# A hybrid encoder layer: where the second product of the fourth and fifth gathered tiles is made

## The chip, the cores and the metric

The kernel runs on one core of a Trainium2 chip. The metric is the device time of one execution in microseconds; the median of three runs of the kernel before is 4287.37 us.

## What is computed

An encoder layer is applied with shared weights to 256 prompt tokens and 1024 sample tokens (width 1024). A recurrent branch and an attention branch are merged; then a channel mixer with product keys picks, for each token, 8 heads x 16 = 128 of 16384 experts. Only the mixer matters here; a tile is 128 tokens.

```python
u = jnp.take(u_tab, eidx, axis=0)      # (128 tokens, 8, 16, 1024)
ve = jnp.take(v_tab, eidx, axis=0)
act = gelu(einsum('td,thkd->thk', zt, u)) * g
return einsum('thk,thkd->td', act, ve)
```

The first product (`u`) gives 128 numbers for each token; the second (`ve`) is a sum of 128 rows weighted by them. The mixer's result is added to the residual and normalised.

## The kernel before

The ten tiles of tokens take two ways through the mixer. Six are gathered: each of a token's 128 expert rows is fetched by index. These are the two prompt tiles (`rP`, here tiles 1 and 2), the first two sample tiles (`r0`, tiles 3 and 4) and the last two (`r1`, tiles 5 and 6). The other four sample tiles (`rd`, 512 tokens) are dense: `weights` (line 1016) turns their picks into a full table of weights, by small matmuls (lines 1034 and 1053), and `dense` (line 1063) multiplies the 512 tokens with all 16384 experts in 128 blocks, 48 fp32r matmuls of 512 columns to a block (lines 140 to 142). `second` adds its results to `acc` on VectorE (line 1096), and `load_split` divides every loaded table block in a high and a low part on ScalarE and VectorE (lines 123 and 124).

For a gathered tile:

- `u_steps`: 128 steps. Each issues one indirect DMA of 512 KB on GpSimd's queue (line 938) and one dot product on VectorE (line 940, with a small read of the accumulator).
- `v_steps`, second product on TensorE: 128 indirect DMAs (line 969); after every fourth, one group of 8 fp32 matmuls (16 records in the trace) with a 128x32 selector that holds the weights (line 976), into `acc` in PSUM. Before it, the 128x128 weights are transposed on TensorE (line 954).
- `v_slots`, the same on VectorE: after every DMA (line 994) one multiply-add of 128x1024 (line 996). A route with the key `"acc"` takes this way. It yields after every second DMA.

All these tiles, and `gffn`, `gfin`, `y` and `x2r`, share one ring of 7 buffers (`ring`, line 925), handed out in the order of the program text; a gather can be issued when the buffer seven back is free. `experts` pairs the second product of a tile with the first of the next one:

```python
def experts(routes):
    prev = None
    for r in routes + [None]:
        us = u_steps(r) if r else iter(())
        vs = (v_slots if "acc" in prev else v_steps)(prev) if prev else iter(())
        while us or vs: ...          # one step of each in turn
        prev = r
```

A scheduler puts the instructions of all stages on each engine's queue when the program is built, by a timeline of its own and with the text's order as priority; the steps of the second product have a higher one. Each engine then runs its queue strictly in that order. So the gathers, which come after `merge` in the text, run beside the attention and merge stages, and those of tiles 5 and 6 beside `weights` and `dense`.

Of the kernel before, what the change touches and what calls it, by code (L numbers as in the profile page):

```python
# [50 lines left out]
def encoder(ctx, tc, I, O, dbg=None):  # L51
# [876 lines left out]
    def u_steps(route):  # L928
        tt, gw, ei = route["tt"], route["gw"], route["ei"]
        zs = pe_.tile([P, D], F32, name="zs", tag="zs")  # L930
        nc.gpsimd.dma_start(zs, x2d[tt:tt + P])
        gffn = ring("gffn")
        nc.sync.dma_start(gffn, I["norm_ffn"].partition_broadcast(P))
        nc.vector.scalar_tensor_tensor(out=zs, in0=zs, scalar=route["rt"], in1=gffn, op0=OP.mult, op1=OP.mult)
        dots = pe_.tile([P, P], F32, name="dots", tag="dots", bufs=2)
        for s in range(P):
            ug = ring("ug")
            nc.gpsimd.indirect_dma_start(out=ug, out_offset=None, in_=I["peer_u"],  # L938
                                         in_offset=bass.IndirectOffsetOnAxis(ap=ei[:, s:s + 1], axis=0))
            nc.vector.scalar_tensor_tensor(out=ug, in0=ug, scalar=1.0, in1=zs, op0=OP.mult, op1=OP.mult,  # L940
                                           accum_out=dots[:, s:s + 1])
            yield
        act = pe_.tile([P, P], F32, name="act", tag="act", bufs=2)
        nc.scalar.activation(out=act, in_=dots, func=AF.Gelu)
        nc.vector.tensor_tensor(act, act, gw.rearrange("p h k -> p (h k)"), op=OP.mult)
        route["act"] = act
        yield
# [162 lines left out]
# [5 lines that stand above are left out]
            while us or vs:  # L1115
                if us and next(us, "end") == "end":
                    us = None
                if vs:
                    with tc.high_priority():
                        if next(vs, "end") == "end":  # L1120
                            vs = None
            prev = r
# [82 lines left out]
    r0 = []  # L1205
# [24 lines left out]
    tctx.close()  # L1230
    rd, r1 = rs[:ND // P], rs[ND // P:]
    vp = ctx.enter_context(tc.tile_pool(name="VA", bufs=1, side="right"))
    for r in r1:
        r["acc"] = vp
    experts(r0 + r1)
    acc = ctx.enter_context(tc.tile_pool(name="DA", bufs=1, side="left")).tile([P, ND // P, D], F32, name="acc")
    up = ctx.enter_context(tc.tile_pool(name="DU", bufs=1, side="left"))
    dense(rd, zt, acc, up, up0, psum_pool(ctx, "psS", 3, "left"), psum_pool(ctx, "psV", 3, "left"))
# [77 lines left out]
```

## Time and profile before

| | |
|---|---|
| median of 3 runs | 4287.37 us (4286.51 to 4300.59) |
| profiled execution | 4300.6 us, span 4298.8 us |
| TensorE busy | 3802.2 us, 88% of the span |
| VectorE busy | 3234.1 us, 75% |
| GpSimd busy | 1818.6 us, 42% |
| ScalarE busy | 1559.9 us, 36% |
| DMA | 1263.92 MB, mean 294 GB/s |

The profiled execution is the slowest of the three by 13 us. Busy shares are means over stages with different limits; the stage of `dense` fills the last 1.5 ms. A matmul's listed duration overlaps with the next one's, so a count of matmuls in a stretch tells its rate better than the busy time.

### The profile page before, as it was taken

The numbers are of one execution on the slowest core, as the hardware profiler recorded it, in microseconds if no ns is written. First come the engines' busy times: TensorE is split into PE (matmuls) and PEld (weight loads), VectorE is DVE, ScalarE is ACT, GpSimd is POOL, SyncE is SP. The second block draws the span as 40 slices with busy tenths as digits, with TensorE's granted clock in tenths as the row PEclk, the third lists the DMA queues.
The fourth block names the chain that finished last, engine by engine and source line by source line (L and its number), as shares of the span: only waits on it lengthen the run. The fifth ranks groups of instructions, "written<-read, shape, count | busy, mean of one in ns | idle before, by whom it ended". The sixth has DMA issues, their size and how long they took to land.

```text
span 4298.8 us, 55005 instructions
## 1 busy us (share of the span) xinstructions
PE 3802.2 (88%) x18206; PEld 2734.5 (64%) x18206; DVE 3234.1 (75%) x8002; ACT 1559.9 (36%) x2600; POOL 1818.6 (42%) x1565
## 2 busy tenths in 40 slices
PE   6998999997777988877988489999999999899998
PEld 5777777775434753345644155677777877777786
DVE  4637988567988773986679985567668999999954
ACT  5555455454233214431201187522222222222232
POOL 0000644334444343774545512344446556666500
PEclk9999999998888999888999688999999999999999
DMA  5455899889999987998988847899999999999941
GB/s 160 123 183 152 324 344 343 315 305 319 318 311 313 323 312 272 328 339 326 334 293 285 292 181 292 325 322 339 334 333 356 339 358 362 365 364 346 326 140 64
DMA packets 508318, 1263.92 MB, mean 294 GB/s; under 512 B 49920, under 2 KB 203136, under 8 KB 505984
## 3 DMA queue, kind: packets, MB, share of 16 engines
q0 software_dynamic: 224352, 816.94, 52.9%
q1 hardware_dynamic: 197056, 354.05, 24.2%
q10 hardware_dynamic: 86624, 89.40, 6.1%
q8 instruction: 144, 2.36, 0.2%
q14 instruction: 142, 1.16, 0.1%
HBM read 1165.05 MB, written 95.16 MB: 293 GB/s over the span
## 4 chain that ended last, share of the span: by engine, by line
PE 55%; DMA 13%; DVE 12%; issue 12%; ACT 4%; POOL 2%; SPq 0%; another core or an unknown queue 0%; POOLq 0%; ACTq 0%; DVEq 0%
PE pm L140 12%; PE pm L141 11%; PE pm L142 11%; PE pm L138 7%; DMA vg<-peer_v,eit 5%; PE acc L976 5%; DVE ug L940 4%; DMA ug<-peer_u,ei 3%; PE pm L1053 3%; POOL ug L938 1%; PE pm L1034 1%; PE pm L437 1%; DVE vacc L996 1%; POOL vg L969 1%; PE pm L624 1%
## 5 line engine op out<-in xcount | busy, mean ns | idle before, releaser
L938 POOL DMA_INDIRECT ug<-peer_u,ei x768 | 908.9, 1184 | 800.8 <-DVE ug L940 334.2
L940 DVE SCALAR_TENSOR_TENSOR ug<-ug,zs 128x1024 f32<-128x1024 f32 x768 | 931.5, 1220 | 252.6 <-DMA ug<-peer_u,ei 189.3
L969 POOL DMA_INDIRECT vg<-peer_v,eit x512 | 540.7, 1056 | 752.8 <-DVE ug L940 308.9
L994 POOL DMA_INDIRECT vg<-peer_v,ei x256 | 354.7, 1385 | 207.0 <-DVE vacc L996 120.3
L141 PE MATMUL pm<-vl,ah 128*128 128x512 f32 x1024 | 405.1, 397 | 22.8 <-DVE vl L124 22.8
L140 PE MATMUL pm<-zth,uh 128*128 128x512 f32 x1024 | 406.3, 397 | 8.7 <-ACT ge L1080 6.0
L142 PE MATMUL pm<-zth,ul 128*128 128x512 f32 x1024 | 405.2, 396 | 0.0
L141 PE MATMUL pm<-ztl,uh 128*128 128x512 f32 x1024 | 404.8, 395 | 0.0
L976 PE MATMUL acc<-vg,zt 128*32 128x512 f32 x2048 | 284.6, 679 | 133.7 <-DMA vg<-peer_v,eit 132.8
L142 PE MATMUL pm<-vh,al 128*128 128x512 f32 x1024 | 400.6, 394 | 0.0
L140 PE MATMUL pm<-vh,ah 128*128 128x512 f32 x1024 | 374.9, 398 | 11.3 <-DVE acc L1096 5.5
L996 DVE SCALAR_TENSOR_TENSOR vacc<-vg,act,vacc 128x1024 f32<-128x1024 f32 x256 | 327.7, 1280 | 3.0 <-DMA vg<-peer_v,ei 0.9
L138 PE MATMUL pm<-xg,wraw 128*128 128x256 f32 (+1 forms) x1024 | 295.2, 441 | 4.1 <-DVE sr L855 4.1
L123 ACT CAST uh<-uraw 128x1024 fp32r<-128x1024 f32 x128 | 134.5, 1051 | 432.5 <-PE pm L141 413.2
L123 ACT CAST vh<-vraw 128x512 fp32r<-128x512 f32 x256 | 157.5, 618 | 352.0 <-DMA vraw<-peer_v 257.3
L140 PE MATMUL pm<-hh,wh 128*128 128x512 f32 x672 | 269.9, 402 | 5.0 <-ACT gt L240 3.0
L141 PE MATMUL pm<-hl,wh 128*128 128x512 f32 x672 | 268.3, 399 | 0.0
L142 PE MATMUL pm<-hh,wl 128*128 128x512 f32 x672 | 266.3, 396 | 0.0
L138 PEld LDWEIGHTS pm<-xg,wraw 128*128 128x128 f32 x1024 | 193.2, 194 | 80.6 <-issue 56.9
L141 PEld LDWEIGHTS pm<-vl,ah 128*128 128x128 f32 x1024 | 194.0, 189 | 75.1 <-DVE vl L124 31.5
L140 PEld LDWEIGHTS pm<-vh,ah 128*128 128x128 f32 x1024 | 194.1, 190 | 66.4 <-DVE acc L1096 14.1
L140 PEld LDWEIGHTS pm<-zth,uh 128*128 128x128 f32 x1024 | 192.2, 188 | 64.6 <-ACT ge L1080 11.4
(368 smaller groups left out, 7502.1 us busy)
## 6 DMA issues: line engine op xcount, KB each, us to landing
uraw<-uT SPq DMA_DIRECT2D x128, 512.0 KB
vraw<-peer_v SPq DMA_DIRECT2D x256, 256.0 KB
wraw<-wi SPq DMA_DIRECT2D x84, 512.0 KB
gd<-gs ACTq DMA_DIRECT2D x16, 2048.0 KB
g<-gd ACTq DMA_DIRECT2D x32, 1024.0 KB
wraw<-wq SPq DMA_DIRECT2D x48, 512.0 KB
wraw<-wo SPq DMA_DIRECT2D x24, 512.0 KB
ug<-peer_u,ei POOLq DMA_INDIRECT x768
```

Of the source, the lines that this page charges most:

```text
L123: nc.scalar.copy(hi, src)
L138: nc.tensor.matmul(out, w[0], x[0], start=start, stop=stop)
L140: nc.tensor.matmul(out, w[0], x[0], start=start, stop=False)
L141: nc.tensor.matmul(out, w[0], x[1], start=False, stop=False)
L142: nc.tensor.matmul(out, w[1], x[0], start=False, stop=stop)
L938: nc.gpsimd.indirect_dma_start(out=ug, out_offset=None, in_=I["peer_u"], in_offset=bass.IndirectOffsetOnAxis(ap=ei[:, s:s + 1], axis=0))
L940: nc.vector.scalar_tensor_tensor(out=ug, in0=ug, scalar=1.0, in1=zs, op0=OP.mult, op1=OP.mult, accum_out=dots[:, s:s + 1])
L969: nc.gpsimd.indirect_dma_start(out=vg, out_offset=None, in_=I["peer_v"], in_offset=bass.IndirectOffsetOnAxis(ap=eit[:, t:t + 1], axis=0))
L976: nc.tensor.matmul(acc[g_ * 32:(g_ + 1) * 32, n * 512:(n + 1) * 512], zt[:, h, g_, i], v_[:, n * 512:(n + 1) * 512], start=b == 0 and i == ...
L994: nc.gpsimd.indirect_dma_start(out=vg, out_offset=None, in_=I["peer_v"], in_offset=bass.IndirectOffsetOnAxis(ap=ei[:, s:s + 1], axis=0))
L996: nc.vector.scalar_tensor_tensor(out=acc, in0=vg, scalar=act[:, s:s + 1], in1=acc, op0=OP.mult, op1=OP.add)
L1053: nc.tensor.matmul(pm[:, j * P:(j + 1) * P], ol[:, j], oh[:, j], start=True, stop=True)
```

## The change

Only the last gathered tile keeps its second product on VectorE, and the list of four tiles is given to `experts` in two calls. Between the calls there is no pairing: tile 4's second product comes alone, then tile 5's first product alone.

```diff
     vp = ctx.enter_context(tc.tile_pool(name="VA", bufs=1, side="right"))
-    for r in r1:
+    for r in r1[1:]:
         r["acc"] = vp
-    experts(r0 + r1)
+    experts(r0)
+    experts(r1)
     acc = ctx.enter_context(tc.tile_pool(name="DA", bufs=1, side="left")).tile([P, ND // P, D], F32, name="acc")
```

The order of the stages of tiles 3 to 6, before: first 3; first 4 with second 3; first 5 with second 4; first 6 with second 5 (VectorE); second 6 (VectorE). After: first 3; first 4 with second 3; second 4; first 5; first 6 with second 5 (TensorE); second 6 (VectorE). All queues are the same up to the end of the second product of tile 3.

GpSimd's queue at that end, before (line 982 and 1014 belong to tile 3's output, line 931 loads tokens for tile 5):

```order
L982 DMA x2r<-x2d 128x1024
L931 DMA zs<-x2d 128x1024
L1014 DMA y<-y 128x1024
L938 DMA ug<-peer_u,ei 128x1024
L969 DMA vg<-peer_v,eit 128x1024
```

The same place after:

```order
L931 DMA zs<-x2d 128x1024
L969 DMA vg<-peer_v,eit 128x1024 x17
L1014 DMA y<-y 128x1024
L969 DMA vg<-peer_v,eit 128x1024 x111
L982 DMA x2r<-x2d 128x1024
L938 DMA ug<-peer_u,ei 128x1024 x10
L1014 DMA y<-y 128x1024
L938 DMA ug<-peer_u,ei 128x1024 x119
```

The alternation of `ug` (tile 5) and `vg` (tile 4) has become one run of 128 `vg` and then one run of `ug`.

VectorE's queue in the middle of `dense`, before, where `ug` is tile 6 and `vacc` tile 5:

```order
L1096 TENSOR_TENSOR acc<-pm,acc 128x512
L996 SCALAR_TENSOR_TENSOR vacc<-vg,act,vacc 128x1024
L1082 TENSOR_TENSOR ge<-ge,g 128x512 x2
L124 TENSOR_TENSOR ul<-uraw,uh 128x1024
L940 SCALAR_TENSOR_TENSOR ug,dots<-ug,zs 128x1024
L996 SCALAR_TENSOR_TENSOR vacc<-vg,act,vacc 128x1024
L160 TENSOR_TENSOR al<-ge,ah 128x512 x2
L124 TENSOR_TENSOR vl<-vraw,vh 128x512
L996 SCALAR_TENSOR_TENSOR vacc<-vg,act,vacc 128x1024
```

After, while tile 5's dot products run alone (this stretch now lies early in `dense`):

```order
L1082 TENSOR_TENSOR ge<-ge,g 128x512
L940 SCALAR_TENSOR_TENSOR ug,dots<-ug,zs 128x1024 x2
L124 TENSOR_TENSOR vl<-vraw,vh 128x512
L160 TENSOR_TENSOR al<-ge,ah 128x512
L940 SCALAR_TENSOR_TENSOR ug,dots<-ug,zs 128x1024
L1082 TENSOR_TENSOR ge<-ge,g 128x512
L124 TENSOR_TENSOR ul<-uraw,uh 128x1024
L124 TENSOR_TENSOR vl<-vraw,vh 128x512
L940 SCALAR_TENSOR_TENSOR ug,dots<-ug,zs 128x1024
```

The 128 multiply-adds of tile 5 are gone from this queue; what stands between the dense operations is one kind of gathered work at a time.

TensorE's queue behind the transposition of tile 4's weights, at the start of `weights`, after the change:

```order
L1053 MATMUL pm<-oh,ol 128x128 x4
L1034 LDWEIGHTS cs
L1034 MATMUL pm<-cbk,cs 128x512
L976 MATMUL acc<-vg,zt_3898 32x512 x8
L1034 LDWEIGHTS cs
L1034 MATMUL pm<-cbk,cs 128x512
L1053 MATMUL pm<-oh,ol 128x128 x4
```

Before, no group of line 976 stands among the first 60 of the 128 such pieces of `weights`, and 6 groups in all of it; after, 17 of tile 4's 32 groups. Tile 5's 32 groups now stand between matmuls of `dense`, where there were none.

## Rows read from the trace of the kernel before

**Rows 1.** The page's slices, 40 equal parts of the span, busy tenths.

```profile
PE   6998999997777988877988489999999999899998
...
DVE  4637988567988773986679985567668999999954
...
DMA  5455899889999987998988847899999999999941
```

**Rows 2.** Tile views: engine, operation, count; least/median/most ns; first and last start.

```profile
L954 PE MATMUL acc<-ident,act x4: 270/302/448, 771.0 to 2484.9; 128*128 128x128 f32 x4
...
L976 PE MATMUL acc<-vg,zt x2048: 592/592/1064, 797.4 to 3242.3; 128*32 128x512 f32 x187
...
L996 DVE SCALAR_TENSOR_TENSOR vacc<-vg,act,vacc x256: 1269/1279/1315, 3252.9 to 4077.7; 128x1024 f32<-128x1024 f32 x128
...
L940 DVE SCALAR_TENSOR_TENSOR ug<-ug,zs x768: 1159/1219/1296, 446.4 to 3789.1; 128x1024 f32<-128x1024 f32 x192
...
L1010 ACT ACTIVATE sq<-vacc x2: 1056/1058/1060, 3657.8 to 4079.0; 128x1024 f32<-128x1024 f32 x2
```

**Rows 3.** Windows of the last six stretches: busy of each engine, PE clock, DMA share, GB/s.

```profile
2490.00:2745.00 255.00, 239.91 (x1391) 152.78 (x1391) 169.21 (x459) 198.95 (x276) 54.62 (x57) 0.93 0.67 252
2745.00:2800.00 55.00, 54.10 (x248) 40.69 (x247) 31.04 (x46) 17.57 (x24) 20.38 (x18) 1.00 0.96 352
2800.00:3200.00 400.00, 398.17 (x1874) 295.46 (x1873) 264.44 (x413) 108.87 (x164) 187.43 (x170) 1.00 0.93 331
...
3300.00:3660.00 360.00, 336.69 (x1413) 265.99 (x1412) 339.72 (x425) 97.17 (x146) 214.69 (x169) 0.98 0.97 354
3660.00:3790.00 130.00, 120.68 (x503) 95.52 (x503) 125.83 (x212) 36.76 (x55) 87.56 (x66) 0.98 0.99 367
3790.00:4080.00 290.00, 282.66 (x1195) 223.31 (x1194) 277.04 (x306) 83.15 (x126) 179.28 (x123) 0.99 0.96 344
4100.00:4260.00 160.00, 160.00 (x697) 130.45 (x696) 75.94 (x105) 48.87 (x74) 0.00 (x0) 1.00 0.33 104
```

**Rows 4.** Windows of line 976 alone, the selector products of the gathered rows.

```profile
2490.00:2745.00 255.00, 11.54 (x96) 2.50 (x96) 0.93 0.67 252
...
2800.00:3200.00 400.00, 40.40 (x336) 8.77 (x336) 1.00 0.93 331
```

**Rows 5.** Timeline of TensorE around one line 976 group: start, length, instruction.

```profile
3146.87 0.39 PE L141 MATMUL pm<-ztl,uh 128*128 128x512 f32 x1
3147.19 1.93 PE L976 MATMUL acc<-vg,zt 128*32 128x512 f32 x16
3149.04 0.50 PE L142 MATMUL pm<-zth,ul 128*128 128x512 f32 x1
3149.38 0.39 PE L140 MATMUL pm<-zth,uh 128*128 128x512 f32 x1
```

**Rows 6.** Waits of TensorE from 3300 to 4080: total us, times, longest.

```profile
PE pm L141 <- DVE vl L124: 22.8, 16, 4.3
PE pm L140 <- ACT ge L1080: 6.0, 6, 1.8
```

**Rows 7.** Window of line 940 alone while dot products run by themselves; two records each.

```profile
3660.00:3790.00 130.00, 77.00 (x127) 0.98 0.99 367
```

**Rows 8.** VectorE groups by line, 3790 to 4080, the last tile's second product.

```profile
L996 DVE SCALAR_TENSOR_TENSOR vacc<-vg,act,vacc 128x1024 f32<-128x1024 f32 x128 | 163.8, 1280 | 1.2
```

**Rows 9.** Waits of TensorE in the weights stretch, 2490 to 2745.

```profile
PE pm L1034 <- DMA cs<-codes: 7.6, 2, 4.5
PE pm L1034 <- ACT gs L1054: 5.6, 5, 4.0
```

**Rows 10.** Waits of TensorE from 1380 to 1700, tile 2's second product alone.

```profile
PE acc L976 <- DMA vg<-peer_v,eit: 25.5, 13, 4.1
```

**Rows 11.** Waits of TensorE from 2490 to 3250.

```profile
PE acc L976 <- DMA vg<-peer_v,eit: 1.8, 1, 1.8
```

**Rows 12.** Waits of TensorE from 1930 to 2490.

```profile
PE acc L976 <- DMA vg<-peer_v,eit: 88.5, 21, 14.9
```

## The prediction

> **What bounds the kernel now.** I read the page's slices first: over the last third TensorE is at 9 tenths nearly everywhere, VectorE climbs to 9 in the slices behind the middle of that third, and the DMA engines are at 9 up to the last three slices [rows 1]. So three resources are nearly full at once, and the question is which one ends each stretch. The tile views date the stretches. Tile 4's weights are transposed at 2484.9 us, its second product on TensorE ends at 3242; the multiply-adds on VectorE run from 3253 to 4078, and the squares of the two finished tiles at 3657.8 and 4079.0 say that tile 5's end near 3660 and tile 6's near 4080; the last dot product is at 3789 [rows 2]. With these dates I asked for a table by stretch [rows 3].
>
> Its last row is the yardstick. From 4100 to 4260 `dense` is alone: 697 matmuls in 160 us, 0.2296 us each, PE never idle. For every other stretch I count the dense matmuls, multiply by 0.2296, and what is left of the stretch is either line 976 or loss.
>
> - 2800 to 3200, tile 5's dot products beside tile 4's second product on TensorE: 1874 records, of which 336 are line 976 [rows 3, 4]. 1538 x 0.2296 = 353.1 us; 46.9 us are left, 1.8 of them idle.
> - 3300 to 3660, tile 6's dot products beside tile 5's multiply-adds: 1413 x 0.2296 = 324.4; lost 35.6 us. VectorE is busy 339.7 of 360.
> - 3660 to 3790, dot products alone: 503 x 0.2296 = 115.5; lost 14.5. VectorE 125.8 of 130.
> - 3790 to 4080, tile 6's multiply-adds alone: 1195 x 0.2296 = 274.4; lost 15.6. VectorE 277.0 of 290 [rows 3].
>
> So TensorE sets the end, and from 3300 to 4080 it loses 65.7 us in all. What it waits for there is VectorE first: 22.8 us for the low part of a table block (line 124), 6.0 for ScalarE's `ge` [rows 6]; the rest of the loss is a clock of 0.98 and short gaps at issue. Before 3300, with the second product on TensorE, nothing is lost.
>
> **The change, term by term.** It adds matmuls to the engine that sets the end and takes work from one that makes it wait; the sum is about these two.
>
> *Tile 5's second product on TensorE: 32 groups of line 976.* Two ways to price one. By the stretch: (398.2 - 353.1) / 21 = 2.15 us, as 336 records are 21 groups of 16. By one group in the timeline: the dense matmul ahead starts at 3146.87, the second one behind it at 3149.38; without the group these two starts would lie 0.46 us apart, they lie 2.51 apart, so the group took 2.05 [rows 5]. I take 2.1: **+67 us** (66 to 69). There is no idle time beside it to hide in, since in its new place, as in 2800 to 3200, TensorE would be at 398 of 400.
>
> Here is the one rule I weigh. The row shows 0.32 us from the last dense start to the group's first, where 0.23 is usual, 1.85 us from the group's start to the next dense start, and 0.34 to the one behind: about 0.2 us of the 2.05 lie at the two borders [rows 5]. The Trainium skill (TensorEngine Tiling (Array Packing), Key Properties) says that a change of the tiling mode, not of the tile alone, drains the engine, and a group of 128x32 among 128x128 matmuls changes it twice. The trace agrees in kind. By the row without its borders 32 groups would be 59 us, with them 67; the rule speaks against the change by those 8.
>
> *Tile 5's multiply-adds leave VectorE.* In the trace, tile 6's take 163.8 us at 1.280 us each [rows 8]; tile 5's are as many. With them goes the mixed stretch. Tile 6's dot products then stand beside line 976, as tile 5's did from 2800 to 3200, where VectorE is busy 264.4 of 400 and TensorE loses nothing. So the 35.6 us of the mixed stretch and the 14.5 us of tile 6's solitary dot products (these are left alone because the multiply-adds go two at a time, so tile 5's are done when tile 6's are halfway) are given back: **-50 us**.
>
> *Tile 5's dot products now come alone, beside dense.* This stretch is new. By the new order it spans some 1246 dense matmuls, 286 us at the full rate. VectorE needs 128 x 1.21 us = 155 for the dots (77.0 us for 63.5 of them, two records each) [rows 7] and, at 75.9 per 160 us [rows 3], 136 for dense, 291 us together: over-full. The nearest rows: dots alone cost 14.5 us per 63.5, that is 29 per 128; multiply-adds alone 15.6 per 128. I take the middle, **+22 us** (15 to 29). Tile 6's own 15.6 us stay as they are: same instructions, same place in dense (blocks 84 to 112 in both orders), with 16 blocks to go behind them.
>
> *Tile 4's second product moves forward.* Before, 6 of its 32 groups lie in `weights` (96 records) [rows 4]; after, 17. 11 x 2.1 = 23 us leave dense and enter `weights`: zero in the sum, except where they fall into idle time. TensorE is busy 239.9 of 255 there [rows 3], waiting 7.6 us for the `cs` load and 5.6 for ScalarE's copy [rows 9]. If TensorE comes later, part of this has arrived; but `cs` and the copy follow from its own progress, so part comes back. Between 0 and 15.1 I take half: **-8 us**. The groups may also wait for their rows, as tile 2's did when its second product ran alone, 25.5 us in 13 waits [rows 10], or hardly, as tile 4's did beside tile 5's dots, 1.8 us [rows 11]. The load on the transfers is nearest to the second: **+5 us**, within 2 to 25. The dots that leave `weights` relieve VectorE, which was at 169 of 255 and not the limit: nothing.
>
> *Small things.* Tile 5's sum of `acc` and residual on VectorE (line 983) is one instruction, about as long as a multiply-add, and the transposition of its weights (line 954, 0.3 us [rows 2]) waits for the last dot product with dense matmuls queued behind it: a few us at most, within the range. DMA: not a byte more or less, the same 256 gathers for each tile; the ring and the two stream borders are as between tiles 1 to 4.
>
> **Sum.** 67 - 50 + 22 - 8 + 5 = **+36 us**. The profiled execution would go from 4300.6 to 4337; it is 13 us over the median, and the same step on the median gives 4287.4 + 36 = **4323 us**. A measurement of this kernel tells about 0.5%, 21 us, from no change; this is 0.8%.
>
> **Rivals.**
>
> *The losses belong to the transfers, not to VectorE: a little faster.* The three lossy stretches have a DMA share of 0.96 to 0.99, the lossless one 0.93 [rows 3], and PE's wait for `vl` has a load in front of it. The change moves 11 groups, 44 gathers of 0.5 MB = 23 MB, into `weights`, where the share is 0.67; at 350 GB/s that is 66 us of transfer out of the full stretches. If this is what counts, neither tile 5's dots nor tile 6's multiply-adds lose anything, and the filled waits of `weights` are worth all 15: 67 - 50 - 16 - 15 = -14 (nothing for tile 5's dots, no 15.6 for tile 6), 4273 us. It decides if the DMA share beside tile 5's dots is under 0.95. Against it: while VectorE is 95% and more busy, the transfers' relief has no room to show, and the named releaser is VectorE's.
>
> *Gathers alone stall TensorE: slower by more.* TensorE's queue is strict, so a group of line 976 whose rows are late stops dense and `weights` too. From 1930 to 2490 it waited so for 88.5 us, 21 times, 4.2 us each [rows 12]. By the new order tile 4's last 15 groups stand some 35 dense matmuls apart; with the group's own time that is 8.0 + 2.1 = 10.1 us for four gathers, 2.5 us each. The transfers have kept up with more: GpSimd's 170 instructions from 2800 to 3200 are one in 2.35 us [rows 3]. So the stretch should hold. If it doesn't, 10 waits of 4.2 us in place of my 5 us give +37 on top: 4360 us. It decides if a gather lands later than 2.5 us behind the one before it, over the length of the stretch.
>
> *The change doesn't do what it says* is ruled out by the order, which shows the moves.
>
> **Chances.** The sum as worked out (4304 to 4340): 0.53, of which 0.08 lies under 4309, within 0.5%. Transfers (4256 to 4300): 0.22, of which 0.08 is faster by over 0.5%. Stalls (4341 to 4375): 0.17. None of these: 0.08, spread as 0.02, 0.03, 0.03. So faster 0.10, same 0.25, slower 0.65. The range leaves out the lower part of the transfers' case and the upper half of the stalls', with the last 0.08 some 0.2: 4268 to 4360. The likeliest case's own range is 4304 to 4340.
>
> **What the profile after would show.** `weights` takes some 15 us longer, with 272 records of line 976 in it. Then tile 5's dots alone, 270 to 310 us long, some 22 us more than its dense matmuls need at 0.2296, with VectorE over 95%. Then about 590 us of tile 6's dots beside line 976, at 470 records per 100 us and no loss. Then tile 6's multiply-adds with some 16 us lost. The forecast is wrong if the second stretch loses nothing or twice as much, if line 976 waits for its gathers in `weights` or early in dense, or if a group costs other than 2.1 us.

## The result and the profile after

The change makes the kernel slower: 4318.99 us, median of 4 runs (4311.5 to 4323.62), beside 4286.94 us for the kernel before (4 runs, 4285.91 to 4300.59), a ratio of 1.0066 with an interval of 1.004 to 1.0091. That is 32 us between the medians, and 28 us (17 to 39) by the ratio. The two profiled executions, 4323.62 and 4300.6 us, are 23 us apart.

From the page of the changed kernel, the busy line and two of the rows by slice, which answer to [rows 1]:

```profile
PE 3837.2 (89%) x18719; PEld 2739.2 (63%) x18719; DVE 3087.6 (71%) x7892; ACT 1560.9 (36%) x2600; POOL 1779.4 (41%) x1565
...
DVE  4637987567987774886679974348886666689964
...
DMA  5464999889999888998987878889989999999951
```

VectorE has 147 us less to do, TensorE 35 more. VectorE's solid run of nines over the last quarter is broken up: three eights (tile 5's dot products alone), five sixes (line 976 beside tile 6's dot products), then an eight and two nines with tile 6's multiply-adds. The transfers stay at 8 or 9 tenths through all of this, up to the last two slices, as before.

The tile views of `vg` in the changed kernel (columns as in [rows 2]): line 976 has 512 records more and ends 573 us later; one tile is left on line 996, and it ends 46 us later.

```profile
L976 PE MATMUL acc<-vg,zt x2560: 592/592/1063, 797.1 to 3815.7; 128*32 128x512 f32 x197
...
L996 DVE SCALAR_TENSOR_TENSOR vacc<-vg,act,vacc x128: 1270/1279/1318, 3824.4 to 4123.6; 128x1024 f32<-128x1024 f32 x128
```

These dates cut the changed kernel into the stretches that the prediction spoke of. The windows view of them, with the columns of [rows 3]:

```profile
2490.00:2756.00 266.00, 253.24 (x1555) 151.65 (x1555) 141.12 (x408) 200.23 (x276) 68.23 (x71) 0.95 0.76 276
2756.00:2925.00 169.00, 167.37 (x831) 115.90 (x832) 66.89 (x96) 46.36 (x68) 55.95 (x55) 1.00 0.86 304
2925.00:3217.00 292.00, 278.43 (x1170) 222.95 (x1169) 263.30 (x431) 79.61 (x120) 179.50 (x136) 0.98 0.96 350
3217.00:3816.00 599.00, 592.44 (x2788) 438.15 (x2786) 394.80 (x618) 161.83 (x244) 282.02 (x251) 1.00 0.92 328
3816.00:4124.00 308.00, 308.00 (x1335) 249.94 (x1332) 289.08 (x331) 89.71 (x136) 168.76 (x129) 1.00 0.96 341
```

And the same for line 976 alone, as in [rows 4]:

```profile
2490.00:2756.00 266.00, 35.23 (x272) 7.37 (x272) 0.95 0.76 276
2756.00:2925.00 169.00, 28.86 (x240) 6.26 (x240) 1.00 0.86 304
...
3217.00:3816.00 599.00, 61.77 (x512) 13.35 (x512) 1.00 0.92 328
```

With the prediction's yardstick (a stretch, less 0.2296 us for each dense matmul, less 2.1 us for each 16 records of line 976), the loss in each stretch is:

| stretch of the changed kernel | dense matmuls | groups | loss, us | before |
|---|---|---|---|---|
| 2756 to 2925, tile 4's last 15 groups | 591 | 15 | 1.8 | not there |
| 2925 to 3217, tile 5's dots alone | 1170 | 0 | 23.4 | 2.8 (beside tile 4's groups) |
| 3217 to 3816, tile 6's dots, tile 5's groups | 2276 | 32 | 9.2 | 35.6 + 14.5 |
| 3816 to 4124, tile 6's multiply-adds | 1331 | 0 | 1.9 | 15.6 |
| together | | | 36.3 | 68.5 |

The account between the two profiles: 32 groups of 2.1 us, +67.2; losses beside `dense`, -32.2; `dense` starts at 2755.9 instead of 2742.0 us, +13.9, but 11 groups (23.1 us) have left it for `weights`, so -9.2. Together +25.8, where the executions differ by 23.

What ended PE's waits in the changed kernel, first from 2925 to 3217, then from 3217 to 3816 (microseconds, times, longest):

```profile
PE pm L140 <- ACT vh L123: 4.7, 1, 4.7
PE pm L140 <- ACT ge L1080: 3.4, 2, 2.9
PE pm L141 <- DVE vl L124: 3.2, 1, 3.2
PE pm L140 <- DVE acc L1096: 2.3, 2, 1.9
...
PE acc L976 <- DMA vg<-peer_v,eit: 6.1, 3, 3.5
```

Beside tile 5's dots the waits are spread over ScalarE and VectorE. They make 13.6 of the 23.4 us lost there. The rest goes with matmuls that took longer: the mean granted clock of the stretch was 0.98, so in parts of it TensorE ran at the lower of its two levels, 1.2 GHz. Behind a wait of 3.15 us that ended at 3133.8, for example, matmuls started 0.43 us apart for some 3 us. Finer windows of the stretch show when the loss comes:

```profile
2975.00:3025.00 50.00, 50.00 (x218) 40.64 (x217) 44.69 (x72) 12.44 (x19) 29.74 (x24) 1.00 0.97 354
3025.00:3075.00 50.00, 50.00 (x217) 40.43 (x216) 46.15 (x73) 14.28 (x22) 28.85 (x21) 1.00 0.94 334
3075.00:3125.00 50.00, 48.14 (x200) 38.45 (x200) 43.40 (x71) 14.59 (x21) 28.61 (x22) 0.97 0.95 342
3125.00:3175.00 50.00, 46.31 (x193) 36.71 (x192) 46.16 (x75) 13.16 (x20) 32.71 (x25) 0.97 0.96 350
3175.00:3217.00 42.00, 33.98 (x132) 26.23 (x131) 36.17 (x61) 10.55 (x18) 26.39 (x19) 0.92 0.98 356
```

The first 100 us shown are at the full rate of 217 records in 50 us, with VectorE at 89 to 92%; then the rate falls to 200, 193 and, in a last window of 42 us, 132, and VectorE is no busier than before. A loss that grows while nothing in the mix changes looks like a reserve being used up, not like an engine that is too slow from the start.

The trace shows such a reserve. VectorE writes `vl`, the low part of half a table block for the second product of `dense` (line 124), ahead of the matmuls that read it (line 141, four to a write). Windows of this tile alone, busy time of PE, PEld and VectorE:

```profile
2925.00:2975.00 50.00, 10.67 (x28) 5.07 (x27) 4.03 (x6) 1.00 0.98 366
2975.00:3025.00 50.00, 13.91 (x36) 6.75 (x36) 4.10 (x6) 1.00 0.97 354
3025.00:3075.00 50.00, 10.21 (x26) 4.88 (x26) 4.79 (x7) 1.00 0.94 334
```

In the first 100 us TensorE starts 64 of these matmuls, the worth of 16 writes, and VectorE makes 12. Counted through the trace (writes made, less a quarter of the matmuls started), the stock is 5.9 in the mean from 2925 to 2975, 2.9 in the next 50 us, 1.5 in the third, and 1.1 from 3075 on, where the loss is. In the kernel before it falls in the same way: 5.6 from 3250 to 3300, 2.4 from 3300 to 3400, 1.2 from 3400 to 3790. The experiments took this up.

### The profile page after: what moved, and what is told of

Same layout as the page of the kernel before. It is cut to its first block, busy times and chain, and to the rows that moved or that the text cites. A ratio compares the mean times of both kernels' runs of the same rounds, so it can differ in the third digit from the quotient of the medians.

```text
span 4321.9 us, 55859 instructions
## 1 busy us (share of the span) xinstructions
PE 3837.2 (89%) x18719; PEld 2739.2 (63%) x18719; DVE 3087.6 (71%) x7892; ACT 1560.9 (36%) x2600; POOL 1779.4 (41%) x1565
## 4 chain that ended last, share of the span: by engine, by line
PE 40%; issue 12%; DMA 9%; POOL 4%; DVE 4%; ACT 1%; POOLq 0%; SPq 0%; DVEq 0%; ACTq 0%
PE pm L140 8%; PE pm L142 8%; PE pm L141 8%; PE acc L976 5%; DMA vg<-peer_v,eit 5%; PE pm L138 5%; PE pm L1053 3%; POOL ug L938 3%; DMA ug<-peer_u,ei 3%; PE pm L1034 2%; DVE ug L940 2%; PE pm L624 1%; PE pm L618 1%; POOL vg L969 1%; PE pm L437 0%
## 5 line engine op out<-in xcount | busy, mean ns | idle before, releaser
L938 POOL DMA_INDIRECT ug<-peer_u,ei x768 | 923.5, 1202 | 760.4 <-DVE ug L940 369.7
L969 POOL DMA_INDIRECT vg<-peer_v,eit x640 | 673.4, 1052 | 993.5 <-PE acc L976 507.5
L976 PE MATMUL acc<-vg,zt 128*32 128x512 f32 x2560 | 342.4, 657 | 145.8 <-DMA vg<-peer_v,eit 145.5
L140 PE MATMUL pm<-vh,ah 128*128 128x512 f32 x1024 | 392.8, 395 | 7.3 <-ACT vh L123 4.7
L976 PEld LDWEIGHTS acc<-vg,zt 128*32 128x32 f32 x2560 | 70.6, 115 | 317.9 <-DMA vg<-peer_v,eit 174.3
L1096 DVE TENSOR_TENSOR acc<-pm,acc 128x512 f32<-128x512 f32 x256 | 172.4, 686 | 111.5 <-PE pm L142 105.3
L124 DVE TENSOR_TENSOR ul<-uraw,uh 128x1024 fp32r<-128x1024 f32 x128 | 156.5, 1223 | 101.3 <-ACT uh L123 86.1
```

The costliest lines, as they stand in the source:

```text
L124: (eng or nc.vector).tensor_tensor(lo, src, hi.bitcast(F32), op=OP.subtract)
L140: nc.tensor.matmul(out, w[0], x[0], start=start, stop=False)
L969: nc.gpsimd.indirect_dma_start(out=vg, out_offset=None, in_=I["peer_v"], in_offset=bass.IndirectOffsetOnAxis(ap=eit[:, t:t + 1], axis=0))
L976: nc.tensor.matmul(acc[g_ * 32:(g_ + 1) * 32, n * 512:(n + 1) * 512], zt[:, h, g_, i], v_[:, n * 512:(n + 1) * 512], start=b == 0 and i == ...
L1096: nc.vector.tensor_tensor(acc[:, t, ns], pm, acc[:, t, ns], op=OP.add)
```

## The experiments

The first three take the change and its terms apart; the next two try the two suspects for the losses; the rest try a theory that came out of these. The kernel before ran beside each of them on the same chip; ratios are to it. Of the kernels whose edit is against the changed kernel, the changed kernel's 1.0066 is the number to compare with.

### The split alone

Both last tiles stay on VectorE; the list goes to `experts` in two calls.

```diff
-    experts(r0 + r1)
+    experts(r0)
+    experts(r1)
```

> The list is split in two calls, but tiles 5 and 6 both keep their second product on VectorE. By terms, as the trace after has them: tile 5's dot products alone cost 23 us, the groups that move into the weights stage give back some 12, the mixed stretch and the last multiply-adds stay as they were: +11 us, 4298 us. Rival, TensorE's groups of tile 5 are the whole cost: no change, 4287 us. Rival, the split is the whole cost: +30 us, 4317 us.

Measured: 4320.15 us (7 runs), ratio 1.0061 (1.0037 to 1.0084). The split alone costs as much as the whole change, which is the second rival's number; my sum was 15 us short by the ratio. The windows of tile 5's dots alone, of tile 6's dots beside tile 5's multiply-adds, and of tile 6's dots alone:

```profile
2920.00:3200.00 280.00, 270.12 (x1133) 216.26 (x1132) 257.41 (x422) 76.99 (x116) 174.41 (x133) 0.97 0.97 352
3200.00:3594.00 394.00, 359.91 (x1493) 281.58 (x1492) 379.18 (x476) 102.01 (x153) 243.86 (x194) 0.98 0.99 364
3594.00:3727.00 133.00, 119.50 (x485) 94.20 (x484) 124.02 (x211) 36.15 (x55) 86.98 (x67) 0.95 0.98 363
```

They lose 19.9, 51.2 and 21.6 us (with tile 6's multiply-adds 14.5 and the first stretch 5.3, 112.5 in all, 44 more than before; 18 came back because 11 groups went into `weights` and `dense` started only 4.7 us later). I had taken the mixed stretch's 35.6 us as a property of its instructions. They are the same kinds here and cost 51.2.

### TensorE alone

Tile 5's second product on TensorE, one call as before.

```diff
-    for r in r1:
+    for r in r1[1:]:
         r["acc"] = vp
```

> One call as before, but tile 5's second product on TensorE. By terms: +69 for 32 groups, +6 for late gathers, -50 for the mixed stretch, -14 for the last multiply-adds, which lost nothing in the trace after: +11 us, 4298 us. Rival, the groups are the whole cost: +30 us, 4317 us. Rival, the split is the whole cost: no change or faster, 4287 us or less.

Measured: 4297.22 us (12 runs), ratio 1.0015 (0.9998 to 1.0032), as expected. The windows of tile 5's dots beside tile 4's groups, then of tile 6's dots beside tile 5's groups:

```profile
2744.00:3250.00 506.00, 505.67 (x2374) 375.89 (x2373) 327.74 (x512) 142.61 (x213) 227.54 (x209) 1.00 0.94 334
3250.00:3838.00 588.00, 584.07 (x2752) 431.19 (x2751) 389.91 (x607) 157.56 (x235) 280.76 (x255) 1.00 0.94 335
```

1.8 and 6.5 us lost, and 1.8 beside tile 6's multiply-adds: 10 in place of 68.5. So the 67 us of added matmuls are nearly paid back. By the ratios the split alone costs some 26 us, TensorE alone 6, and both together 28: the parts don't add, since the mixed stretch that the split made worse is the one that the other part removes.

### Tile 5's groups made twice

The changed kernel, each of tile 5's 32 groups issued a second time on the same rows.

```diff
+                        for rep in range(2 if "twice" in route else 1):
                             for n in range(2):
```

> The changed kernel with each of tile 5's 32 groups of line 976 made twice (that tile's second product is doubled). Price theory: 32 x 2.1 = 67 us more than the changed kernel, 4386 us. If a group were mostly hidden, or if only waits made its price, less than 30 us more.

Measured: 4401.9 us (4 runs), ratio 1.0256 (1.0221 to 1.0291), 82 us over the changed kernel by the ratios, 67 expected; the two profiled executions are 75 us apart. PE's wait for gathered rows from 3200 to 3900:

```profile
PE acc L978 <- DMA vg<-peer_v,eit: 15.6, 8, 4.9
```

32 x 2.1 = 67, and 9.5 us more of waiting than the 6.1 of the changed kernel, are 77, near the 75 of the profiles. A group is a cost in full, with nothing to hide it.

### Tile 5's multiply-adds halved

The kernel before; tile 5's 128 multiply-adds work on 512 of 1024 columns. The gathers are unchanged.

```diff
-            nc.vector.scalar_tensor_tensor(out=acc, in0=vg, ...)
+            hc = slice(0, D // 2 if "half" in route else D)
+            nc.vector.scalar_tensor_tensor(out=acc[:, hc], in0=vg[:, hc], ...)
```

> The kernel before, with tile 5's 128 multiply-adds on half the columns (the other half of that tile's second product is left out); every gather keeps its size. VectorE theory: 128 x 0.6 us = 77 us less on VectorE in the mixed stretch, so most of the 50 us lost there and of the 16 us lost beside the last multiply-adds are gone: 4230 to 4250 us. Transfer theory: the bytes are the same, so no change, 4287 us.

Measured: 4287.53 us (12 runs), ratio 0.9994 (0.9976 to 1.0012). Nothing gained: a miss for the theory that the prediction stood on. The windows of the mixed stretch and of the dots alone, then a wait of PE and two of VectorE from 3228 to 3758:

```profile
3228.00:3640.00 412.00, 393.59 (x1656) 310.58 (x1648) 330.50 (x513) 110.31 (x165) 229.53 (x201) 0.98 0.98 364
3640.00:3758.00 118.00, 101.42 (x394) 78.38 (x395) 110.06 (x180) 27.78 (x42) 76.54 (x62) 0.90 0.97 355
...
PE pm L140 <- ACT vh L123: 14.5, 9, 2.7
...
DVE acc L1097 <- PE pm L142: 35.9, 26, 4.7
DVE ul L124 <- ACT uh L123: 33.4, 21, 5.3
```

VectorE is down to 80% in the mixed stretch and TensorE still loses 32.6 us there and 27.5 behind it. The fifth of its time that VectorE has free is in good part waiting in its own queue's order, 35.9 us for TensorE and 33.4 for ScalarE, where the kernel before has 10.4 and 9.1 (3300 to 3790). The DMA share is 0.98 at 364 GB/s, so the transfers may stand right behind VectorE; this run does not show it, since the build had also ordered things otherwise: VectorE's queue has 25 to 28 gathered operations for eight writes of `vl` (four blocks) where before had 23 to 27.

### Multiply-adds and gathers halved

The same with half rows gathered for tile 5's second product (half the bytes, the same number of gathers).

```diff
+            if "half" in route:
+                nc.gpsimd.indirect_dma_start(out=vg[:, 0:512], ...,
+                                             in_=I["peer_v"].rearrange("e (n j) -> (e n) j", n=2), ...)
+                nc.vector.scalar_tensor_tensor(out=acc[:, 0:512], in0=vg[:, 0:512], ...)
```

> The kernel before, with tile 5's gathers of the second product fetching half a row and its multiply-adds on half the columns (half of that tile's second product is left out). The run with half the multiply-adds alone changed nothing. If transfers and VectorE limit the mixed stretch together, one right behind the other, taking half from both frees it: of 66 us lost from the mixed stretch on at least 40 are gone, 4230 to 4250 us. If neither limits it, 4287 us.

Measured: 4282.02 us (12 runs), ratio 0.9975 (0.9954 to 0.9995), another miss. Windows of the mixed stretch, and from 3300 to 3600 what PE and VectorE waited for:

```profile
3400.00:3500.00 100.00, 91.12 (x387) 71.73 (x386) 83.74 (x128) 25.80 (x41) 63.83 (x55) 1.00 0.88 293
3500.00:3600.00 100.00, 90.78 (x372) 71.46 (x371) 82.16 (x132) 27.17 (x43) 59.24 (x50) 0.96 0.87 298
...
PE pm L140 <- DVE acc L1103: 5.2, 5, 3.0
PE pm L142 <- DVE ul L124: 5.1, 3, 2.5
...
DVE ug L940 <- DMA ug<-peer_u,ei: 36.6, 25, 3.7
```

VectorE at 82 to 84%, the DMA share at 0.87 to 0.88, and TensorE makes 372 to 387 matmuls in 100 us instead of 435. TensorE waits for VectorE, and VectorE's queue stands 36.6 of 300 us before dot products whose rows have not landed; in the kernel before it never waits for them in these 300 us. What had changed is the order: with lighter work the build packs 28 gathers into four blocks of `dense`, where before had 25. That gave the theory of spacing: the order of the build is fixed for each engine, and where it puts more gathers between the dense operations than are worked off in the time of those blocks, the dense operations behind them come late, whichever resource is the one that is short. Why rows land late here at a share of only 0.87 stays open. Half the bytes with VectorE's work kept whole was not measured.

### A ring of six, everywhere

A gather can be issued when the buffer six back is free, so the order can't pack them so closely. The kernel before, and then the changed kernel, with

```diff
-RING = 7
+RING = 6
```

> The kernel before with a ring of 6 buffers in place of 7, same work. The order made for it has 20 to 22 gathers to four blocks of dense in the mixed stretch where it had 25. Density theory (TensorE loses where the order packs more gathers than land in the time of its blocks): most of the 66 us go, some 10 come back at the end, where the last multiply-adds now reach block 128, and in the weights stage: 4235 to 4265 us. Rival, the losses come from the mixed work itself: 4285 us or more, since fewer buffers hide less.

> The changed kernel with a ring of 6. Density theory: the 23 us lost beside tile 5's dot products and the 9 beside tile 6's are thinner packed and mostly gone, 4285 to 4305 us. Rival: 4319 us or more.

Measured: 4358.93 us (6 runs), ratio 1.0154 (1.0126 to 1.0182), and 4413.85 us (6 runs), ratio 1.0276 (1.0245 to 1.0307). Both missed, and by their numbers both are the rival's: the stages ahead of `dense` became slower too. The first dense matmul starts at 2800.5 us in the one and 2807.8 in the other (2742.0 before), and in the second tile 6's multiply-adds end at 4365, beyond the last matmul of `dense`, which would cover them. In the first, `dense` itself took 1507 us from first to last matmul, 10 less than before. And in the place in question, the mixed stretch of the first of the two:

```profile
3500.00:3600.00 100.00, 100.00 (x435) 81.20 (x434) 93.51 (x120) 28.03 (x44) 58.36 (x43) 1.00 0.95 343
3600.00:3700.00 100.00, 100.00 (x433) 80.89 (x432) 91.51 (x116) 29.66 (x44) 52.53 (x42) 1.00 0.94 337
```

The same kinds of instruction, VectorE at 92 to 94%, and 0.1 and 0.6 us lost. To test this apart from the earlier stages, the ring had to be narrowed late.

### One buffer held beside dense

Seven buffers up to tile 5's first dot; from there to tile 6's last multiply-add one of them is held by a tile that is written once and read at the end. First in the kernel before, then in the changed one.

```diff
+        if "hold" in route:
+            hold = ring("hold")
+            nc.gpsimd.memset(hold[:, 0:1], 0.0)
+            route["hold"].append(hold)
...
+        if route is r1[-1]:
+            nc.vector.tensor_copy(act[:, 0:1], r1[0]["hold"][0][:, 0:1])
...
+    r1[0]["hold"] = []
```

> The kernel before, but from tile 5's first dot to tile 6's last multiply-add one of the ring's seven buffers is held (written once, read at the end), so that gathers beside the dense products have six; the earlier stages keep seven. The order of the build then has 39 to 45 gathers in 8 dense blocks of the mixed stretch, where before had 44 to 52, and 43 beside the lone dots, where before had 50; the number of gathers and of VectorE's operations is unchanged. Theory of spacing: 22 gathers or fewer in 4 blocks cost TensorE nothing, so the 35.6, 14.5 and 15.6 us fall to about 10 together, 5 are given back to late gathers of line 976 on tile 4: 4230 to 4255 us. Rival, each gather (or its VectorE operation) costs its share wherever it stands: the same 68 us spread over more blocks, 4280 to 4295 us.

> The changed kernel, with one of the ring's seven buffers held in the same way from tile 5's first dot to tile 6's last multiply-add. The order has 42 and 43 gathers in 8 blocks beside tile 5's lone dots where the changed kernel has 49 and 51; beside tile 6's dots and line 976 it keeps its 43 to 44 gathers of both kinds. Theory of spacing: the 23.4 us beside tile 5's dots fall to under 5, but line 976 has a buffer less for its four gathers and may wait longer, by 0 to 10: 4295 to 4310 us. Rival, each gather costs its share wherever it stands: 4315 to 4325 us.

Measured: 4271.86 us (6 runs), ratio 0.9948 (0.9929 to 0.9966), beside 4295.03 for the kernel before on that chip; and 4333.05 us (6 runs), ratio 1.0092 (1.0072 to 1.0112). The first gained 22 us, a number between the two theories'; the second lost some 11 more than the changed kernel, outside both. Windows of the first, tile 5's dots beside tile 4's groups and then the mixed stretch:

```profile
2900.00:3298.00 398.00, 378.07 (x1744) 273.92 (x1744) 244.79 (x381) 103.05 (x155) 177.45 (x161) 0.99 0.89 311
3298.00:3700.00 402.00, 399.11 (x1719) 321.74 (x1718) 374.42 (x482) 112.97 (x170) 234.98 (x180) 1.00 0.97 348
```

The mixed stretch lost 7.3 us where before lost 35.6 in a shorter one, as the theory of spacing has it. But the stretch ahead of it lost 29.0, where before lost next to nothing. 12.3 of these are named waits for the rows of line 976 (`vg`, 7 waits), so six buffers seem too few where a group needs four of them at once. The second kernel shows the same, 5.4 us lost beside tile 5's dots (23.4) and 33.0 beside line 976 (9.2), but there only 7.4 are named waits for `vg`, and the rest is spread over ScalarE, VectorE and a lower clock (0.99). The theory had the place right and left out this price.

### One buffer held where no group needs it

Held from tile 6's first dot (kernel before), or from tile 5's first dot to its last (changed kernel):

```diff
-    r1[0]["hold"] = []
+    r1[1]["hold"] = []
```

> The kernel before, with one of the ring's seven buffers held only from tile 6's first dot to its last multiply-add, so that tile 5's dots and line 976 on tile 4 keep seven. In the kernel that held it from tile 5's first dot on, the mixed stretch lost 6.8 us (35.6 in the profile before), the lone dots 8.5 (14.5), the multiply-adds 13.9 (15.6), but 28 us were lost beside line 976 on tile 4, where before lost 3. The order here has 39 to 46 gathers in 8 blocks of the mixed stretch and 46 beside the lone dots. Theory of spacing: the mixed stretch loses 7 to 10 us, the rest about 22 as in that kernel, nothing more beside line 976: 4240 to 4262 us. Rival, each gather costs its share wherever it stands: 4275 to 4295 us.

> The changed kernel, with one of the ring's seven buffers held from tile 5's first dot to its last dot, and free again for line 976 on tile 5. The order has 42 and 43 gathers in 8 blocks beside tile 5's lone dots, where the changed kernel has 49 and 51. In the kernel that held it to the end, those dots lost 5.4 us (23.4 in the changed kernel) and line 976 on tile 5 lost 29 us (9.2). Theory of spacing: the dots lose about 5, line 976 about 9 again: 4298 to 4310 us. Rival, each gather costs its share wherever it stands: 4315 to 4325 us.

Measured: 4272.35 us (12 runs), ratio 0.9953 (0.993 to 0.9975); and 4305.47 us (12 runs), ratio 1.0017 (0.9996 to 1.0038), which is 21 us under the changed kernel by the ratios, as expected. The window of tile 5's dots in the second kernel:

```profile
2932.00:3214.00 282.00, 280.97 (x1212) 227.04 (x1211) 254.44 (x415) 81.72 (x122) 160.89 (x126) 1.00 0.96 345
```

42 dense matmuls more in 10 us less than in the changed kernel, and the loss is 3.7 us instead of 23.4, with the same VectorE share (90%) and the same DMA share (0.96). The window holds 119 of the 128 dots; the others now stand behind it, beside line 976, where 5.8 us are lost (9.2). This is the cleanest single reading: the 22 us that the prediction gave to tile 5's dots are a matter of how closely they stand. The stock of `vl` is drawn down here too, from 5.8 in the first 50 us to 1.4 in the last 82, so this spacing is not shown to run without loss for longer. The first kernel gained 20 us, where 25 to 47 were expected; the windows of its tile 6 dots alone and its multiply-adds say why:

```profile
3700.00:3834.00 134.00, 125.92 (x527) 98.97 (x526) 123.67 (x207) 36.16 (x53) 81.48 (x65) 0.99 0.98 357
3834.00:4119.00 285.00, 277.14 (x1166) 218.06 (x1165) 273.29 (x302) 82.29 (x125) 176.21 (x123) 0.99 0.96 345
```

13.0 and 17.3 us are still lost there. Its order has 46 gathers in eight blocks beside the dots, where before had 50, and 48 in the eight blocks in which the multiply-adds begin.

### Two buffers held

```diff
-            hold = ring("hold")
+            for _ in range(2):
+                hold = ring("hold")
```

> As the kernel that held one buffer of the ring from tile 6's first dot to its last multiply-add, but two are held, five remain. The order has 37 to 41 gathers in 8 blocks of the mixed stretch and 34 to 37 beside the lone dots; the multiply-adds that follow have 45, 40 and 39. The gathers end about 8 blocks later than with one held, still before the last dense block. Theory of spacing: with one held, 8.9, 13.0 and 17.3 us were lost in the three stretches; here about 3, 3 and 12, so 20 us less than with one held and 40 to 50 less than before: a ratio of 0.988 to 0.992. Rival, each gather costs its share wherever it stands (and one buffer held gained for another reason): no better than with one held, 0.995 to 1.000.

Measured: 4238.33 us (6 runs), ratio 0.9869 (0.9846 to 0.9891): 56 us less than before, a little more than expected, and faster than both kernels. Windows of the mixed stretch with the dots behind it, then of tile 6's multiply-adds:

```profile
3240.00:3860.00 620.00, 616.44 (x2661) 500.23 (x2660) 570.12 (x785) 183.69 (x278) 332.49 (x260) 1.00 0.94 337
3860.00:4150.00 290.00, 289.29 (x1249) 234.11 (x1248) 273.09 (x301) 83.89 (x126) 170.55 (x125) 1.00 0.97 343
```

9.0 and 3.2 us lost. Every instruction of the kernel before is there; VectorE is 92 to 94% busy and the transfers at 0.94 to 0.97 for 900 us on end, and TensorE loses 1.5 and 1.1%. Nothing of the work was taken away: it was spread over more blocks, up to 4156 us instead of 4078. With 0.9 us beside tile 4's groups (2800 to 3240) the losses are 13.1 us where before had 68.5, which makes 55 of the 56 us. The stock of `vl` is 4.2 in the first window, where it was 1.5 and 1.1 in before, and 2.0 in the second.

### All of them together

For each stretch in which every gather has a VectorE operation behind it, the trace gives the number of those operations for 192 dense matmuls (four blocks, 44.1 us at the full rate) and the loss as a share of the stretch:

| gathers in four blocks | kernel and stretch | loss |
|---|---|---|
| 18.2, 18.5, 18.7, 18.7 | multiply-adds: one held to tile 5's last dot; changed; TensorE alone; changed with one held to the end | 0.4, 0.6, 0.6, 0.5% |
| 18.4, 19.4 | two held: mixed with dots behind; multiply-adds | 1.5, 1.1% |
| 18.9, 19.8 | tile 5's dots: one held to the last dot; to the end | 1.3, 2.0% |
| 19.4, 19.4 | mixed: one held from tile 6's first dot; from tile 5's | 2.0, 1.8% |
| 20.0, 20.0, 20.7 | multiply-adds: split alone; one held from tile 5's first dot; before | 4.9, 4.6, 5.4% |
| 20.3, 22.4 | tile 6's dots: one held from tile 5's first dot; from tile 6's | 4.7, 9.7% |
| 21.0, 21.5 | tile 5's dots: changed; split alone | 8.0, 7.1% |
| 21.2 | multiply-adds: one held from tile 6's first dot | 6.1% |
| 23.1, 24.2 | before: mixed; tile 6's dots | 9.9, 11.2% |
| 24.8, 25.1 | split alone: mixed; tile 6's dots | 13.0, 16.3% |
| 17.8, 22.7, 29.2 | tile 5's multiply-adds halved: tile 6's multiply-adds; mixed; tile 6's dots | 1.4, 7.9, 23.3% |

The loss begins between 19 and 20 and grows from there, whatever the mix of dots and multiply-adds. Where half of the gathers go to line 976 instead, 21.6 (changed) and 21.9 (TensorE alone) cost 1.5 and 1.1%. A part of the rise is in the measure itself, since a stretch that loses has fewer dense matmuls to divide by; the buffers held are the evidence that the order is the cause.

VectorE's own work tells much the same. Its busy time, divided by what TensorE needs for the same matmuls at the yardstick's price, is 105, 109 and 101% in the three lossy stretches of before and 98% beside tile 5's dots in the changed kernel (91% with one buffer held). Of the stretches above with full work, none under 96% lost more than 2.0%, and none from 98% up less than 4.6%. So for the full work, spacing is how much of VectorE a block of `dense` asks for, and these runs don't part the two. Only the two runs with halved work lost much below that: 7.9% at 87% (the mixed stretch above), 11 and 15% at 94 and 96% (half rows too, 3400 to 3600). There VectorE's queue stood waiting.

## Why the prediction was right, and where it was not

The number, 4323, was 4 us off, and the side was right. That it came so near is in part luck: with the sizes measured, the terms make less, and the medians happen to lie on the high side of the profiles. By its steps:

- *32 groups, +67.* Right; making them twice cost 75 (profiles) to 82 (ratios), of which 9.5 is waiting.
- *-50 given back by the mixed stretch and tile 6's dots.* They are gone; the stretch that took their place loses 9.2, not nothing.
- *Tile 5's dots alone, +22.* Measured 23.4, in a stretch of 292 us (270 to 310 was given). But VectorE is at 90% of the time, not over 95, and its work is 98% of what TensorE needs, not more than all of it. The term was the middle of two neighbours' prices, and neither price is fixed: with one buffer held 119 of the same dots cost 3.7 us. That the middle fitted is luck.
- *Tile 6's multiply-adds, "stay as they are".* This failed: 1.9 us in place of 15.6. In before some 7 of the 15.6 lie in the 20 us at the border to the dots, where the two kinds overlap; and the whole stretch runs at 20.7 gathers in four blocks, after at 18.5. The same instructions have no fixed loss.
- *11 groups into `weights`, -8.* Right: `dense` starts 13.9 us later for 23.1 us of matmuls.
- *Late gathers, +5.* About +8: 9.2 and 1.8 us, less before's 2.8; 6.1 and 1.6 of these are named waits for `vg`.

With these the terms make 67 - 50 + 23 - 14 - 9 + 8 = +25, where +36 was summed and 23 (profiles) to 32 (medians) measured. The step that was off is tile 6's, where a gain of 14 us was put at nothing.

The account of the 65.7 us was short in one place. The waits view names 38.3 us of them: to the 22.8 and 6.0 quoted it adds 4.7 for `vh` and 4.6 for `acc`, and "short gaps at issue" are 0.2. Of the other 27, the granted clock of the three stretches (0.98, 0.98, 0.99) accounts for some 13; the rest is not accounted for.

The reason given for the losses was only half of it. "While VectorE is 95% and more busy, the transfers' relief has no room to show" named VectorE, and by its work for each dense matmul VectorE does sort the stretches with full work. But its busy share does not (90% with 23.4 and with 3.7 us lost), and with tile 5's multiply-adds halved, in an order that the build had packed anew, nothing was gained. The rival, that the losses belong to the transfers, fell too: the share beside tile 5's dots is 0.96, so not under the 0.95 on which it was to be decided; at the same 0.96 tile 6's multiply-adds lost 1.9 us; and with half the bytes gone little was gained. In these kernels with full work both resources are within some per cent of full, and the order asks for more at once than they give in the time of the blocks. Apart from its 67 us of matmuls, the change paid because it thinned the order beside tile 6's dots and multiply-adds, and cost because it packed it beside tile 5's dots. "Gathers alone stall TensorE" did not come: tile 4's last groups alone, early in `dense`, lost 1.8 us, and in `weights` the waits for `vg` are 3.4.

What is short first in a given block is settled only in part. In the kernel before and in the changed one the stock of VectorE's `vl` falls from about 6 to 1, and VectorE waited no more than 1.1 us for what ScalarE makes for it (2925 to 3217, changed kernel), so its own queue sets this. With half rows the stock stays at 4.5 (3300 to 3600), and VectorE's queue stands still for rows that land late, at a share that leaves room.

## What to carry to other kernels

Where several queues are fixed when the program is built, price a stretch by how much work its order puts into each block of the engine that ends it, not by the busy share: with VectorE at 92 and at 94% this kernel lost 1.5% or a tenth of TensorE's time, by the spacing. Before moving work to the engine that sets the end to relieve another (with TensorE alone, 67 us paid for 58 us back), try to spread it: fewer buffers for the prefetch, in that stage only, were worth 56 us in the kernel before, with no work moved. A smaller ring must be tried by place, since six buffers instead of seven cost some 25 us where groups of four are consumed.

## What was not expected of the hardware

- Transfers at a share of 0.94 to 0.97 (337 to 343 GB/s) and VectorE at 92 to 94% were held for 900 us with TensorE at 0.232 to 0.233 us for each 512-column matmul (0.2296 with `dense` alone) and a granted clock of 1.00 (2.4 GHz).
- A stretch that will lose starts at full rate: 100 to 150 us go by (2925 to 3075 beside tile 5's dots, 3250 to 3400 in the kernel before) until the loss shows, and it grows to a tenth and more. In that time the stock of `vl` falls from about 6 to below 2.
- Half the bytes of tile 5's gathers lowered the DMA share in the mixed stretch from 0.97 [rows 3] to 0.87 and the rate to 293 to 298 GB/s, and yet VectorE waited 36.6 us for gathered rows from 3300 to 3600.
- Waits for loads are no sign of loss: ScalarE waited for `vraw` 69 us in the kernel before (3300 to 3790), and 127 us with two buffers held (3240 to 3930), where TensorE lost 9.0 of 620 us.
